# Conditioning projections in rounds of sixteen chunks, four chunks of columns per group of PE columns

## The chip, the cores and the metric

The kernel runs on one core of one Trainium2 chip. Its time is the device time of one launch, in microseconds (us). A core has five engines with queues of their own, which run in order: PE (matmuls; its weight loads are listed as PEld), DVE (vector work), ACT (scalar work), POOL (GpSimd) and SP, which here issues the transfers between main memory (HBM) and the on-chip buffer (SBUF). PE writes into the eight banks of PSUM, and DVE and ACT read results from there. The instructions are ordered on each queue by a scheduler when the program is built, from the order of the code, from priorities (`tc.high_priority`) and from its own simulated times. A tile from a pool with `bufs=n` gets the buffer that was handed out n tiles earlier, and its first writer waits until all readers of that older tile are done.

## What is computed

One inference step of a two-layer decoder for 512 prompt tokens and 8 short sequences of 8 tokens (576 columns in all): a gated delta rule layer (layer A), shared keys and values, and a differential attention layer (layer B). Every norm is shifted and scaled, and every residual gated, by vectors that come from a conditioning input `c`, one row for the prompt and eight for the sequences:

```python
def ada_split(c, w, b, n):
    return jnp.split(c @ w + b, n, axis=-1)

def modulate(x, gain, shift, scale):
    return rms_norm(x, gain) * (1 + scale[:, None, :]) + shift[:, None, :]

shift, scale, gate = ada_split(c, p['ada_w_a'][l], p['ada_b_a'][l], 3)
h = modulate(x, p['norm_a'][l], shift, scale)
```

The three weight matrices have 1024 rows and 3072, 2048 and 3072 columns: 64 chunks of 128 columns. The first 16 (shift and scale of layer A) are needed at once. The change is about the other 48, whose results are first read in the output projection of layer A and later.

## The kernel before

Activations are kept transposed (128 features by 576 columns, eight times). A large projection goes by chunks of 128 output columns (`loadw`, `part`): a raw 512 KB tile `wraw` is loaded, ACT casts it to `whi` (L233), POOL makes the rest `wlo` = `wraw` - `whi` (L234), and PE runs 48 matmuls of 288 columns (L257: for each half of the columns and each of eight row blocks, whi with the high and the low part of the activations, then wlo). There are 105 such chunks in a fixed order of use; `wraw`, `whi` and `wlo` have two buffers each, so the load of a chunk waits for POOL to be done with the chunk before the last.

Layer A (`phase_a`) goes through eight groups of two heads. Strings of letters give the order of the code for a group: `v w z y k q` are projection chunks (v, w, z, y of this group, k and q of the next), `T` and `t` the inverse of a triangular matrix on DVE (`tinv_dve`, L916 and L918 are its inner steps), `P` its completion by small matmuls on PE (`tinv_pe`, L940 to L959, with ACT copies between its stages), `1` and `2` the preparation of the next group (`prep1`: transposes of k and q, L713 to L728, and norms; `prep2`: products of k and q, L757 to L768, from which the next `T` starts), `C` the recurrence over four chunks of the group before, `s r` the eight sequences, `o` its norm and gate, `h` a chunk of the output projection, and `a` one conditioning chunk. `P` takes its PSUM tiles from the pool `pa` (one bank), as the conditioning chunks do; `prep1`, `prep2` and the transposes of v (L788) use the pool `pt` (two banks).

One `a` is `ada_unit`: a 512 KB load into `araw` (L265); eight matmuls (L269), the 32-row conditioning block as weights and 128 columns of the chunk streaming, each on one of the four groups of 32 PE columns, so that the four groups hold four partial sums; an ACT copy out of PSUM (L272); one matmul with a constant of nine columns (L273), which adds up the four partial sums and transposes; a DVE add of the bias (L275) into `mod`.

Of the kernel before, what the change touches and what calls it, by code (L numbers as in the profile page):

```python
# [10 lines left out]
F32 = mybir.dt.float32  # L11
# [4 lines left out]
ALU = mybir.AluOpType  # L16
# [21 lines left out]
VEC = {}  # L38
# [61 lines left out]
    return out  # L100


STEP = 'CvTtwkaaasaazPaqry12o'
STEP0 = 'CTtvaaawazasryakqa12oPa'
STEP7 = 'CTtvswzyaHahhrhhhaahhaaaPoah'
STEP8 = 'CLsaraoaaaaaaaa'


def step_of(i):

    return STEP0 if i == 0 else STEP8 if i == G else STEP7 if i == G - 1 else STEP


CHUNKS = chunk_cols()
WORDER = use_order()
# [91 lines left out]
def scr(K, n):  # L207
    t = K.scr.tile([128, 640], F32, name="scr")
    return t[:, 0:n]
# [48 lines left out]
                               start=(k == 0 and a + b == 0), stop=(k == 7 and a == 1))  # L258


def ada_unit(K, kt, pool, name, raw=None):

    nc = K.nc
    ch = raw or K.araw.tile([128, 8, 128], F32, name="araw")
    nc.sync.dma_start(out=ch[:], in_=K.ada[kt].rearrange("p (k m) -> p k m", m=128))  # L265
    ps = pool.tile([128, 512], F32, name=name)
    for k in range(8):
        j = k % 4
        nc.tensor.matmul(out=ps[32 * j:32 * j + 32, 0:128], lhsT=K.cT[:, k, :], rhs=ch[:, k, :],  # L269
                         start=(k < 4), stop=(k >= 4), tile_position=(0, 32 * j))  # L270
    sb = K.adsb.tile([128, 128], F32, name="adsb")
    nc.scalar.copy(out=sb[:], in_=ps[:, 0:128])  # L272
    nc.tensor.matmul(out=ps[:, 128:137], lhsT=sb[:], rhs=K.asel, start=True, stop=True)  # L273
    v0 = VEC["ada_b"][0] + kt
    nc.vector.tensor_scalar(out=K.mod[:, kt, :], in0=ps[:, 128:137], scalar1=K.vec[:, v0:v0 + 1], scalar2=None,  # L275
                            op0=ALU.add)


def ada_pair(K, k, pool, name, raw):
# [235 lines left out]
def phase_a(K, A, ctx, first):  # L515
    nc = K.nc
    tc = K.tc
    A.rows = ctx.enter_context(tc.tile_pool(name="rows", bufs=1))
    c = load_con(K, A.rows, K.con_in, "mask", "smaskb")
# [10 lines left out]
    def pool(name, bufs):  # L530
        return ctx.enter_context(tc.tile_pool(name=name, bufs=bufs))
# [6 lines left out]
    A.y = pool("y", 1)  # L538
    A.v = pool("v", 1)
    K.araw = pool("araw", 1)  # L540
    K.adsb = pool("adsb", 1)
    A.ln = pool("ln", 1)
    A.gb = pool("gb", 2)
    A.eg = pool("eg", 4)
# [12 lines left out]
    kts = K.kts  # L557

    def ada(raw=None):
        if kts:  # L560
            ada_unit(K, kts.pop(0), K.pa, "pa", raw)
# [7 lines left out]
    ada()  # L569
    ada()  # L570
    prev, cur = None, nxt
    m = 0
    for i in range(G + 1):
        nxt = Group(K, A, i + 1) if i + 1 < G else None
        hot = HP if i == G else 0
        for t in step_of(i):
# [45 lines left out]
            if t == "L":  # L622
                new_h(K)
                out_heads(K, range(8, 14), CUTS)
            if t in "ab":
                ada(A.WFs[0] if t == "b" else None)
        prev, cur = cur, nxt


# [300 lines left out]
def tinv_pe(K, A, ck, WF):  # L930

    nc = K.nc
    XA, XC, WC = A.XA, A.XC, A.WC
    pvz = K.pa.tile([128, 2, 8, 32], F32, name="pa")
    pv, pz = pvz[:, 0], pvz[:, 1]
    V1 = A.ln.tile([128, 8, 32], F32, name="V1", tag="V")
    for s in range(2):
        a, b = 64 * s, 64 * s + 32
        for n in range(8):
            nc.tensor.matmul(out=pv[b:b + 32, n, :], lhsT=ck[a:a + 32, n, b:b + 32], rhs=XC[a:a + 32, n, :],  # L940
                             start=True, stop=True, tile_position=(a, b))
        nc.scalar.activation(out=V1[b:b + 32], in_=pv[b:b + 32], func=AF.Copy, scale=-1.0)
        for n in range(8):
            nc.tensor.matmul(out=pz[a:a + 32, n, :], lhsT=V1[b:b + 32, n, :], rhs=WC[b:b + 32, n, :],
                             start=True, stop=True, tile_position=(b, a))
            if s == 0:
                nc.tensor.matmul(out=pz[b:b + 32, n, :], lhsT=WC[b:b + 32, n, :], rhs=V1[b:b + 32, n, :],
                                 start=True, stop=True, tile_position=(b, b))
        nc.scalar.copy(out=WF[a:a + 32, :, b:b + 32], in_=pz[a:a + 32])
        if s == 0:  # L950
            nc.scalar.copy(out=XA[b:b + 32, :, 0:32], in_=pz[b:b + 32])
    pv2 = K.pa.tile([128, 8, 64], F32, name="pa")
    for n in range(8):
        nc.tensor.matmul(out=pv2[64:128, n, :], lhsT=ck[0:64, n, 64:128], rhs=XA[0:64, n, :],
                         start=True, stop=True, tile_position=(0, 64))
    V2 = A.ln.tile([128, 8, 64], F32, name="V2", tag="V")
    nc.scalar.activation(out=V2[64:128], in_=pv2[64:128], func=AF.Copy, scale=-1.0)
    for n in range(8):
        nc.tensor.matmul(out=pv2[0:64, n, :], lhsT=V2[64:128, n, :], rhs=WF[64:128, n, 64:128],  # L959
                         start=True, stop=True, tile_position=(64, 0))  # L960
# [513 lines left out]
def phase_b(K, ctx, x1, rstd, norm_rest):  # L1474
    nc = K.nc
    tc = K.tc
    P = Ctx()

    def pool(name, bufs):
# [5 lines left out]
    c = load_con(K, one, K.con_in, "amask", "plain")  # L1485
# [11 lines left out]
                            scalar2=None, op0=ALU.mult)  # L1497
# [4 lines left out]
    for t in P.qs + [P.zb]:  # L1502
# [17 lines left out]
                                   op0=ALU.mult, op1=ALU.add)  # L1520
# [15 lines left out]
    for i in (1, 0):  # L1536
# [7 lines left out]
    assert not K.kts  # L1544
    qctx = ExitStack()
    extra_w(K, qctx, "qx", [("b", h * 128) for h in range(2, QH)])
    tiles = []
# [34 lines left out]
    with ExitStack() as pctx:  # L1582
# [10 lines left out]
        n = dict.fromkeys("vzf", 0)  # L1593
# [87 lines left out]
def setup(K, ctx, ins):  # L1681
    nc = K.nc
    tc = K.tc
    K.per = ctx.enter_context(tc.tile_pool(name="per", bufs=1))
    K.wraw = ctx.enter_context(tc.tile_pool(name="wraw", bufs=2))
    K.wq, K.wnext, K.wx = [], 0, {}
    K.g1 = {}
    K.kts = list(range(16, 24)) + list(range(40, 56)) + list(range(24, 40)) + list(range(56, 64))
# [11 lines left out]
    c = load_con(K, K.per, ins["con"], "ident", "asel")  # L1700
# [11 lines left out]
    K.mod = K.per.tile([128, 64, 9], F32, name="mod")  # L1712
    K.wall = ins["wall"]
    K.ada = ins["ada"]
    K.cst_in = ins["cst"]
    K.st_in = ins["st"]
    K.con_in = ins["con"]
# [65 lines left out]
def arrays_of(i):  # L1783
    f = {k: np.asarray(v) for k, v in i.items()}
    xa = np.concatenate([f["x_prompt"].reshape(SEQ, D), f["x_sample"].reshape(NS, D)], 0)
    a = {}
# [6 lines left out]
    a["ada"] = np.ascontiguousarray(ad.reshape(8, 128, 64, 128).transpose(2, 1, 0, 3)).reshape(64, 128, 1024)  # L1793
# [72 lines left out]
```

## Time and profile before

Three runs took 1361.96, 1363.52 and 1375.33 us. The profile is of one further execution.

| what | value |
|---|---|
| median of the runs | 1363.52 us |
| the profiled execution, own time | 1368.16 us |
| its span (first to last instruction) | 1366.4 us |
| mean granted PE clock | 0.953 of full |
| stretch of layer A's groups | about 62 to 760 us |
| conditioning chunks of `ada_unit` in it | 48, from 62 to 676 us |
| `wraw` loads | 105 of 512 KB, median 3.8 us to landing |

A row of instructions gives engine, line, operation, tile written <- tiles read, shape, how many (x), the busy time in us and the mean length of one in ns, then the idle time of the engine just before and what ended it. A row of the timeline gives the start and the length in us. A 32-bit matmul leaves two records (two passes). Matmuls are pipelined, so that two successive starts tell more of what one costs PE than its length.

### The profile page before, as it was taken

What the parts mean: (1) busy time and instruction counts of PE and PEld (TensorE: products, weight loads), DVE (VectorE), ACT (ScalarE), POOL (GpSimd) and SP (SyncE); (2) the same over time, 40 slices, a digit from 0 to 9 for tenths busy, and PEclk for the clock granted to TensorE, in tenths of its full rate; (3) what the DMA queues carried; (4) which work ended last, traced back from release to release, by engine and by line L of the source; (5) the groups of instructions that cost most, each with busy time, mean ns of one, the idle gap of its engine ahead of it and who ended that gap; (6) DMA issues with size and microseconds to landing.
All of it is one profiled execution on the core that took longest, in us unless ns stands there. A gap on an engine that the chain in (4) does not pass through costs nothing.

```text
span 1366.4 us, 31102 instructions
## 1 busy us (share of the span) xinstructions
PE 1256.5 (92%) x11477; PEld 1078.5 (79%) x11477; DVE 961.3 (70%) x2437; ACT 729.1 (53%) x2043; POOL 512.2 (37%) x766
## 2 busy tenths in 40 slices
PE   7989799899899898999889899699999999989988
PEld 4879779688788777978779688599888777767888
DVE  5689986779989788897882668688742466555451
ACT  4566446748576674857643542254444465555440
POOL 4543414224252322424123432945553343423222
PEclk8999889899999999998899899899999999999999
DMA  9353224334334343344444445021777877885333
GB/s 356 134 161 111 83 93 132 112 109 126 134 100 142 118 143 109 116 147 135 125 158 133 149 139 190 31 79 60 263 271 242 260 226 248 284 264 168 114 118 114
DMA packets 79578, 211.63 MB, mean 155 GB/s; under 512 B 13554, under 2 KB 27250, under 8 KB 79426
## 3 DMA queue, kind: packets, MB, share of 16 engines
q1 hardware_dynamic: 79426, 209.64, 47.1%
q8 instruction: 91, 1.49, 0.4%
q14 instruction: 61, 0.50, 0.1%
HBM read 183.76 MB, written 25.84 MB: 153 GB/s over the span
## 4 chain that ended last, share of the span: by engine, by line
PE 53%; DVE 27%; ACT 7%; DMA 5%; issue 5%; POOL 3%; SPq 1%; POOLq 0%; DVEq 0%; ACTq 0%
PE pp L257 26%; DVE y L476 3%; DVE tp L916 3%; PE po L1325 2%; PE pS L1282 2%; DVE XT L918 2%; DMA pg<-ck 2%; PE sc L257 1%; PE pv L1445 1%; PE sc L1405 1%; PE px L1307 1%; PE ps L1023 1%; DMA pg<-cv 1%; PE pa L269 1%; PE pt L757 1%
## 5 line engine op out<-in xcount | busy, mean ns | idle before, releaser
L257 PE MATMUL pp<-hhi,whi 128*128 128x288 f32 x1504 | 460.6, 309 | 29.8 <-ACT hhi L369 12.2
L257 PE MATMUL pp<-hlo,whi 128*128 128x288 f32 x1504 | 456.0, 304 | 2.3 <-DVE hlo L361 1.4
L257 PE MATMUL pp<-hhi,wlo 128*128 128x288 f32 x1504 | 453.5, 302 | 0.3 <-POOL wlo L234 0.3
L234 POOL TENSOR_TENSOR wlo<-wraw,whi 128x1024 fp32r<-128x1024 f32 x105 | 253.4, 2414 | 293.2 <-ACT whi L233 276.5
L257 PEld LDWEIGHTS pp<-hhi,whi 128*128 128x128 f32 x1504 | 285.5, 191 | 48.0 <-ACT hhi L369 12.9
L257 PEld LDWEIGHTS pp<-hlo,whi 128*128 128x128 f32 x1504 | 286.9, 191 | 14.1 <-issue 6.5
L257 PEld LDWEIGHTS pp<-hhi,wlo 128*128 128x128 f32 x1504 | 286.6, 191 | 7.1 <-issue 5.5
L233 ACT CAST whi<-wraw 128x1024 fp32r<-128x1024 f32 x105 | 109.8, 1046 | 104.6 <-PE pp L257 70.2
L476 DVE SCALAR_TENSOR_TENSOR y<-u,vec,y 128x600 f32<-128x600 f32 x96 | 96.4, 1004 | 8.3 <-ACT y L474 7.8
L1051 POOL TENSOR_TENSOR wm<-w,con_mask 96x512 fp32r<-96x512 f32 x32 | 35.4, 1105 | 141.5 <-DVE w L1040 84.5
L916 DVE TENSOR_TENSOR tp<-XT,LA 128x32 f32<-128x32 f32 (+15 forms) x128 | 75.5, 590 | 2.5
L1425 DVE TENSOR_REDUCE mx<-sc 128x1 f32<-128x128 f32 (+3 forms) x64 | 31.4, 491 | 61.1 <-PE sc L1407 61.0
L1252 POOL COPY pg<-ptt 1x1 int32<-1x1 int32 x128 | 27.8, 225 | 104.0 <-PE po L1325 45.4
L918 DVE TENSOR_REDUCE XT<-tp 128x16 f32<-128x32 f32 (+15 forms) x128 | 54.9, 429 | 2.4
L1048 ACT ACTIVATE Ss<-Ss,egl 128x128 f32<-128x128 f32 x128 | 42.2, 395 | 23.7 <-PE ps L1023 23.4
L1325 PE MATMUL po<-pg,pTs 128*8 128x128 f32 x1024 | 42.4, 280 | 4.3 <-DMA pg<-cv 3.8
L1282 PE MATMUL pS<-pg,qs 128*32 128x128 f32 x1024 | 42.5, 278 | 4.2 <-DMA pg<-ck 4.1
L1402 POOL TENSOR_TENSOR qd<-qT,qd 64x128 fp32r<-64x128 f32 x64 | 32.4, 507 | 35.9 <-ACT qd L1401 32.2
L269 PE MATMUL pa<-araw,cT 128*32 128x128 f32 x768 | 35.9, 294 | 8.7 <-DVE mod L275 5.6
L479 ACT ACTIVATE scr<-y 128x600 f32<-128x600 f32 x32 | 22.5, 704 | 36.3 <-DVE y L476 36.0
L1427 ACT ACTIVATE pm<-sc,mx 128x128 f32<-128x128 f32 (+3 forms) x64 | 33.6, 527 | 13.9 <-DVE mx L1425 13.0
L1282 PEld LDWEIGHTS pS<-pg,qs 128*32 128x32 f32 x1024 | 26.8, 109 | 12.8 <-issue 5.1
(455 smaller groups left out, 2772.1 us busy)
## 6 DMA issues: line engine op xcount, KB each, us to landing
wraw<-wall SPq DMA_DIRECT2D x105, 512.0 KB, 3.8
pg<-ck SPq DMA_DIRECT2D x64, 512.0 KB, 5.1
pg<-cv SPq DMA_DIRECT2D x64, 512.0 KB, 4.7
araw<-ada SPq DMA_DIRECT2D x48, 512.0 KB, 3.5
araw<-ada SPq DMA_DIRECT2D x8, 1024.0 KB, 11.9
Ss<-st SPq DMA_DIRECT2D x16, 512.0 KB, 3.7
o_sts<-Ss SPq DMA_DIRECT2D x16, 512.0 KB, 2.9
gb<-gcd SPq DMA_DIRECT2D x16, 288.0 KB, 4.0
```

The costliest lines, as they stand in the source:

```text
L233: nc.scalar.copy(out=hi[:], in_=raw[:])
L234: nc.gpsimd.tensor_sub(out=lo[:], in0=raw[:], in1=hi[:].bitcast(F32))
L257: K.nc.tensor.matmul(out=ps[:, :HT], lhsT=w[a][:, k, :], rhs=h[b][:, k, half * HT:half * HT + HT], start=(k == 0 and a + b == 0), stop=(k ...
L269: nc.tensor.matmul(out=ps[32 * j:32 * j + 32, 0:128], lhsT=K.cT[:, k, :], rhs=ch[:, k, :], start=(k < 4), stop=(k >= 4), tile_position=(0, ...
L476: (nc.gpsimd if j in TAP[K.tapi] else nc.vector).scalar_tensor_tensor(out=y[:, :YW], in0=u[:, j:j + YW], scalar=cw[j], in1=y[:, :YW], op0= ...
L916: nc.vector.tensor_mul(out=tp[:, :, :, :n], in0=XT[:, :, :n].unsqueeze(2).to_broadcast([128, 8, 2, n]), in1=LA[:, i:n, :n].unsqueeze(1).to ...
L918: nc.vector.tensor_reduce(out=XT[:, :, i:n], in_=tp[:, :, :, :n], axis=AX.X, op=ALU.add, negate=True)
L1048: nc.scalar.activation(out=S[:, b, :], in_=S[:, b, :], func=AF.Copy, scale=egl[:, hh, 4 + b:5 + b])
L1051: nc.gpsimd.tensor_mul(out=wm[:], in0=w3[:, a, :].bitcast(F32).unsqueeze(1).to_broadcast([96, 4, 128]), in1=K.smaskb.unsqueeze(2).to_broad ...
L1282: nc.tensor.matmul(out=S[32 * j:32 * j + 32, 128 * pg:128 * pg + 128], lhsT=qs[:, h, :], rhs=kp[:, h, :], start=(hh == 0), stop=(hh == 1), ...
L1325: nc.tensor.matmul(out=po[32 * j:32 * j + 8, hf, :], lhsT=pTs[:, pg, 8 * h:8 * h + 8], rhs=vp[:, h, :], start=False, stop=(pg == NPG - 1 a ...
L1427: nc.scalar.activation(out=p[:, :w], in_=pss[m][:, :w], func=AF.Exp, bias=mx[:, m:m + 1], accum_out=ls[:, qt, m:m + 1])
```

## The change

The 48 chunks go in three rounds of 16. A step (`ada_step`, 24 in all) loads 1 MB: one block of 128 rows of W for the 16 chunks of the round, laid out by the host. It runs four matmuls of 512 columns, one on each group of 32 PE columns, so that each group holds four whole chunks and adds over the eight steps of a round in the one bank of `pa`, which is held through the round. Only the last step of a round copies the bank (ACT, 512 columns, into a tile of the pool `scr`), transposes it in four pieces on PE (L286), and adds the bias on DVE in two pieces. Before, each of the 48 chunks had its own copy, matmul and add.

As `pa` is held, `tinv_pe` takes its two tiles from `pt`. As `araw` is twice as large, `wraw` has one buffer in place of two. Over the eight groups the letter `a` stood 62 times, with two calls ahead of the loop (64 calls, of which the first 48 found work); now it stands 23 times with one call ahead, 24 steps. The other letters keep their order. The 16 first chunks are untouched.

```diff
-STEP = 'CvTtwkaaasaazPaqry12o'
-STEP0 = 'CTtvaaawazasryakqa12oPa'
-STEP7 = 'CTtvswzyaHahhrhhhaahhaaaPoah'
-STEP8 = 'CLsaraoaaaaaaaa'
+STEP = 'CvTtwkasazPaqry12o'
+STEP0 = 'CTtvawazsryakq12oP'
+STEP7 = 'CTtvswzyaHhhrhhhahhPoh'
+STEP8 = 'CLsro'
...
-def ada_unit(K, kt, pool, name, raw=None):
-    ch = raw or K.araw.tile([128, 8, 128], F32, name="araw")
-    nc.sync.dma_start(out=ch[:], in_=K.ada[kt].rearrange("p (k m) -> p k m", m=128))
-    ps = pool.tile([128, 512], F32, name=name)
-    for k in range(8):
-        j = k % 4
-        nc.tensor.matmul(out=ps[32 * j:32 * j + 32, 0:128], lhsT=K.cT[:, k, :], rhs=ch[:, k, :],
-                         start=(k < 4), stop=(k >= 4), tile_position=(0, 32 * j))
-    sb = K.adsb.tile([128, 128], F32, name="adsb")
-    nc.scalar.copy(out=sb[:], in_=ps[:, 0:128])
-    nc.tensor.matmul(out=ps[:, 128:137], lhsT=sb[:], rhs=K.asel, start=True, stop=True)
-    v0 = VEC["ada_b"][0] + kt
-    nc.vector.tensor_scalar(out=K.mod[:, kt, :], in0=ps[:, 128:137], scalar1=K.vec[:, v0:v0 + 1], scalar2=None,
-                            op0=ALU.add)
+def ada_step(K, pool, name):
+    r, k = divmod(K.adn, 8)
+    K.adn += 1
+    ch = K.araw.tile([128, 4, 512], F32, name="araw")
+    nc.sync.dma_start(out=ch[:], in_=K.adb[r, k].rearrange("p (j n) -> p j n", j=4))
+    if k == 0:
+        K.adp = pool.tile([128, 512], F32, name=name)
+    ps = K.adp
+    for j in range(4):
+        nc.tensor.matmul(out=ps[32 * j:32 * j + 32, :], lhsT=K.cT[:, k, :], rhs=ch[:, j, :], start=(k == 0), stop=(k == 7),
+                         tile_position=(0, 32 * j))
+    if k < 7:
+        return
+    sb = scr(K, 512)
+    nc.scalar.copy(out=sb, in_=ps[:])
+    for q in range(4):
+        nc.tensor.transpose(out=ps[:, 128 * q:128 * q + 128], in_=sb[:, 128 * q:128 * q + 128], identity=K.ident)
+    for i in range(2):
+        kt = KTS[ROUND * r + 8 * i]
+        v0 = VEC["ada_b"][0] + kt
+        nc.vector.tensor_add(out=K.mod[:, kt:kt + 8, :].rearrange("p (j q) c -> p j q c", j=2),
+                             in0=fr(ps[:, 64 * i:64 * i + 1], [[32, 2], [128, 4], [1, 9]]),
+                             in1=fr(K.vec[:, v0:v0 + 1], [[4, 2], [1, 4], [0, 9]]))
...
-    pvz = K.pa.tile([128, 2, 8, 32], F32, name="pa")
+    pvz = K.pt.tile([128, 2, 8, 32], F32, name="pt")
...
-    pv2 = K.pa.tile([128, 8, 64], F32, name="pa")
+    pv2 = K.pt.tile([128, 8, 64], F32, name="pt")
...
-    K.wraw = ctx.enter_context(tc.tile_pool(name="wraw", bufs=2))
+    K.wraw = ctx.enter_context(tc.tile_pool(name="wraw", bufs=1))
```

How the change moves instructions is shown at two places. The first is PE around the end of `P` of group 3 and the preparation of group 4 (of groups 0 to 7). Before, the products of `prep2` (L757, tile pt) stand around the last stage of `P` (L959, tile pa), and the transposes of k and q are long past:

```order
L257 MATMUL pp<-hhi,whi 128x288
L257 MATMUL pp<-hlo,whi 128x288
L757 MATMUL pt<-k 128x128
L757 MATMUL pt<-q,k 128x128
L757 MATMUL pt<-k 128x128
L959 MATMUL pa<-WF_131,V_4656 64x64 x8
L757 MATMUL pt<-q,k 128x128
L883 MATMUL ps<-con_ident,osb 128x64
L768 MATMUL pt<-kqs 64x128
L257 MATMUL pp<-hhi,wlo 128x288
```

After, on the same engine, the transposes of k (now L725) stand just ahead of the last stage of `P` (now L971, tile pt):

```order
L260 MATMUL pp<-hhi,whi 128x288
L890 MATMUL ps<-con_ident,ob 128x128 x2
L725 MATMUL pt<-con_ident,k 128x128 x4
L971 MATMUL pt<-WF_131,V_4330 64x64 x8
L890 MATMUL ps<-con_ident,ob 128x128 x2
L260 MATMUL pp<-hlo,whi 128x288
```

Twenty projection matmuls later on PE the transposes of q (L735) and of the sequences' k and q (L740) follow and then `prep2` (L769). The row of a conditioning step (L279, four matmuls) is cut in two here; of the 24 steps, 8 are cut in two parts, 16 stand whole:

```order
L260 MATMUL pp<-hhi,wlo 128x288
L279 MATMUL pa<-araw,cT 32x512 x2
L835 MATMUL pc<-vr,WF_131 128x128 x2
L735 MATMUL pt<-con_ident,q 128x128 x4
L740 MATMUL pt<-con_ident,kqs 128x128
L895 MATMUL ps<-con_ident,osb 128x64
L279 MATMUL pa<-araw,cT 32x512 x2
L843 MATMUL pc<-wv,ckq 128x128 x2
L844 MATMUL pc<-wk,kt 128x256
L1035 MATMUL ps<-Ss,kTm 32x128 x14
L769 MATMUL pt<-k 128x128
```

So `P`, which stood beside the preparation of the next group, now stands ahead of all of it. The second place is SP at the start of the program. Before, the raw tiles of two weight chunks are issued one behind the other:

```order
L283 DMA araw_322<-ada 128x2x1024
L230 DMA wraw<-wall 128x1024 x2
L283 DMA araw_442<-ada 128x2x1024
L283 DMA araw_490<-ada 128x2x1024
L666 DMA cso<-cst 128x4x24 x2
L1017 DMA Ss<-st 128x1024
L283 DMA araw_538<-ada 128x2x1024
L283 DMA araw_586<-ada 128x2x1024
L230 DMA wraw<-wall 128x1024 x2
```

After, one raw tile is issued there, and the second behind all loads of the first sixteen conditioning chunks:

```order
L299 DMA araw_322<-ada 128x2x1024
L233 DMA wraw<-wall 128x1024
L299 DMA araw_442<-ada 128x2x1024
L299 DMA araw_490<-ada 128x2x1024
L678 DMA cso<-cst 128x4x24 x2
L1029 DMA Ss<-st 128x1024
L299 DMA araw_538<-ada 128x2x1024
L299 DMA araw_586<-ada 128x2x1024
L233 DMA wraw<-wall 128x1024
L274 DMA araw<-adb 128x2048
```

The second weight chunk moved from beside the first to behind the last conditioning load.

More of the change, by code (lines that the diff above doesn't have):

```diff
@@ L556, in phase_a, with ada @@
     A.WC = A.ln.tile([128, 8, 32], F32, name="WC")
[L557 to L561, printed above, removed]
+    def ada():
+        ada_step(K, K.pa, "pa")
     nxt = Group(K, A, 0)
@@ L568, in phase_a @@
         nxt.prep2()
-    ada()
     ada()
@@ L624, in phase_a @@
                 out_heads(K, range(8, 14), CUTS)
-            if t in "ab":
-                ada(A.WFs[0] if t == "b" else None)
+            if t == "a":
+                ada()
         prev, cur = cur, nxt
@@ L1543, in phase_b @@
         tabs.append(tab)
-    assert not K.kts
+    assert K.adn == len(KTS) // 2
     qctx = ExitStack()
@@ L1792, in arrays_of @@
     ad = np.concatenate([f["ada_w_a"][0], f["ada_w_kv"], f["ada_w_b"][0]], 1)
-    a["ada"] = np.ascontiguousarray(ad.reshape(8, 128, 64, 128).transpose(2, 1, 0, 3)).reshape(64, 128, 1024)
+    ad = ad.reshape(8, 128, 64, 128)
+    a["ada"] = np.ascontiguousarray(ad[:, :, :16].transpose(2, 1, 0, 3)).reshape(16, 128, 1024)
+    a["adb"] = np.ascontiguousarray(ad[:, :, KTS].reshape(8, 128, 3, 16, 128).transpose(2, 0, 1, 3, 4)).reshape(3, 8, 128, 2048)
     W = {"a": f["w_in_a"][0], "oa": f["w_out_a"][0], "kv": f["w_kv"], "b": f["w_in_b"][0], "ob": f["w_out_b"][0]}
```

6 lines of the change are left out of this document (4 added, 2 removed).

## The prediction

> **What bounds the kernel now.** I read the page's engine table and chain first, then windows, then groups by line, then the timeline of PE and DVE where the edits stand. Engine, busy time, share and instructions; then the shares of the chain of work that ended last:
>
> ```profile
> PE 1256.5 (92%) x11477; PEld 1078.5 (79%) x11477; DVE 961.3 (70%) x2437; ACT 729.1 (53%) x2043; POOL 512.2 (37%) x766
> PE 53%; DVE 27%; ACT 7%; DMA 5%; issue 5%; POOL 3%; SPq 1%; POOLq 0%; DVEq 0%; ACTq 0%
> ```
>
> PE is busy for 92%, yet only 53% of the chain is PE's and 27% is DVE's: a microsecond taken from PE does not arrive whole. By stretch (its length; busy PE, PEld, DVE, ACT, POOL; granted clock; DMA share; GB/s), first all groups of layer A, then its beginning, then one group:
>
> ```profile
> 62.00:760.00 698.00, 640.99 (x5720) 560.06 (x5718) 574.46 (x1449) 429.95 (x1298) 234.63 (x275) 0.95 0.39 124
> 62.00:180.00 118.00, 102.10 (x889) 91.36 (x888) 109.08 (x243) 69.65 (x193) 47.76 (x57) 0.91 0.36 112
> 343.00:421.00 78.00, 73.22 (x710) 65.13 (x712) 69.33 (x180) 54.92 (x170) 27.21 (x35) 0.98 0.41 131
> ```
>
> The first 118 us are led by DVE (109 of 118), later groups by PE (73 of 78) with DVE close behind (69). PE stands idle for 698 - 641 = 57 us in the stage. The conditioning chunks hold these groups there (busy, mean ns, then idle time ahead and what ended it):
>
> ```profile
> L269 PE MATMUL pa<-araw,cT 128*32 128x128 f32 x768 | 35.9, 294 | 8.7 <-DVE mod L275 5.6 <-DMA araw<-ada 3.1
> L273 PE MATMUL pa<-con_ident,adsb 128*128 128x9 f32 x96 | 15.5, 234 | 1.1 <-ACT adsb L272 1.0
> L275 DVE TENSOR_SCALAR mod<-pa,vec 128x9 f32<-128x9 f32 x48 | 10.5, 218 | 4.8 <-PE pa L273 4.7
> ```
>
> **PE work removed.** Pipelined matmuls are priced by how far they push the next start. One chunk's eight matmuls, and then its summing matmul, between projection matmuls:
>
> ```profile
> 61.92 0.29 PE L257 MATMUL pp<-hlo,whi 128*128 128x288 f32 x1
> 62.14 0.64 PE L269 MATMUL pa<-araw,cT 128*32 128x128 f32 x16
> 62.71 0.40 PE L257 MATMUL pp<-hhi,wlo 128*128 128x288 f32 x1
> ...
> 66.39 0.30 PE L257 MATMUL pp<-hhi,wlo 128*128 128x288 f32 x1
> 66.53 0.30 PE L257 MATMUL pp<-hhi,whi 128*128 128x288 f32 x1
> 66.66 0.28 PE L273 MATMUL pa<-con_ident,adsb 128*128 128x9 f32 x2
> 66.80 0.38 PE L257 MATMUL pp<-hlo,whi 128*128 128x288 f32 x1
> 67.02 0.29 PE L257 MATMUL pp<-hhi,wlo 128*128 128x288 f32 x1
> ```
>
> The usual pitch is 66.53 - 66.39 = 0.14. The chunk costs 62.71 - 61.92 - 0.13 = 0.66. From 66.53 to 67.02 are 0.49 with two pitches of 0.13 in them, so L273 costs 0.23. 48 x 0.89 = 42.7 us go.
>
> **PE work added.** The nearest rows to a step of four by 512 columns are the sixteen first chunks (256 columns wide), whose row also shows the same work packed four wide; the others are a chunk that PE's order cuts in two, and four transposes of 128 columns:
>
> ```profile
> 44.51 1.93 PE L287 MATMUL pt<-araw,cT 128*32 128x256 f32 x32
> ...
> 357.08 0.62 PE L269 MATMUL pa<-araw,cT 128*32 128x128 f32 x10
> 358.05 0.42 PE L269 MATMUL pa<-araw,cT 128*32 128x128 f32 x6
> 374.64 0.66 PE L723 MATMUL pt<-con_ident,q 128*128 128x128 f32 x4
> ```
>
> 32 records are two such chunks of eight matmuls in two passes: 0.97 us for 8 x 256 columns, as many as 4 x 512. With the 0.1 that a switch cost above (0.66 against the record's 0.64, and a longer first pass behind it) a step takes 1.07, and 24 take 25.7. The low end is 24 x 0.90 = 21.6, if longer streams hide the weights better; the high end is 24 x 1.93 = 46, if two of the four passes do not overlap; 0.97 is nearest, being of the same columns on the same four groups.
>
> By the order of after, 8 of the 24 steps are cut in two pairs with other matmuls between. The chunk cut above took 0.62 + 0.42 = 1.04 against 0.64 whole, as groups overlap only where they stand together. A cut step then keeps its two pairs busy for a whole stream each: + 0.97, times 8 = 7.8 (from 0, if the neighbours fill in, to 8). Twelve transposes at 0.66 / 4 to 0.27: 2.0 to 3.2, taken 2.6. Added: 25.7 + 7.8 + 2.6 = 36.1; PE saves 6.6.
>
> A rule bears on the step. The Trainium skill, "TensorE: Matmul & The Clock Gate", Part 3 on packing small matmuls, gives 2.38 for three column tiles of 32 by 512, 79% of the ideal 3. By it a step would take 0.97 / 0.79 = 1.23, an estimate, and the sum would rise by 24 x 0.26 = 6. No run here shows four groups at 512 columns; the 128-wide and 256-wide rows agree on almost full overlap (0.64 for 128 x 8, 1.93 for 256 x 16), so I keep 0.97.
>
> **Idle time and other engines.** The waits at L269 of 5.6 (for L275 to leave the one bank) and 3.1 (for `araw`, one buffer) and of 1.1 at L273 are per chunk; three rounds in place of 48 leave few of the first. The loads of 1 MB have a row from the start of the program (median time to landing last):
>
> ```profile
> araw<-ada SPq DMA_DIRECT2D x8, 1024.0 KB, 11.9
> ```
>
> 24 steps in a stage of 698 us stand 29 us apart, so 11.9 is hidden there, as long as two steps stand no closer than that; where the order puts them closer, PE waits for the rest, up to 11 us once a group. I take 6 of 9.8 as saved; 0 is possible, if PE then waits for DVE or for such a load, and 9.8 at most. DVE loses 10.5 for six longer adds (at the 0.22 of L275 to about 0.5: 1.3 to 3), ACT 48 small copies for three. So PE and its waits lose 12.6. What arrives at the end: in the first stretch, where DVE leads, little; some 40 of the 48 chunks stand in groups led by PE, where DVE is 4 us of 78 behind. I take 8; from 0 to 12.6.
>
> **`P` on `pt`, and the preparation behind it.** T is the DVE inverse of group 3 (its first and last inner steps, and the first of group 4); then `P` and the preparation of group 4, in time:
>
> ```profile
> 342.88 0.18 DVE L916 TENSOR_TENSOR tp<-XT,LA 128x32 f32<-128x32 f32 x1
> 369.72 0.68 DVE L916 TENSOR_TENSOR tp<-XT,LA 128x512 f32<-128x512 f32 x1
> 379.00 0.39 PE L273 MATMUL pa<-con_ident,adsb 128*128 128x9 f32 x2
> 383.42 0.69 PE L940 MATMUL pa<-XC,ckq 32*32 32x32 f32 x16
> 395.20 0.27 PE L728 MATMUL pt<-con_ident,kqs 128*128 128x128 f32 x1
> 408.62 1.14 PE L959 MATMUL pa<-WF,V 64*64 64x64 f32 x16
> 410.22 1.66 DVE L761 SCALAR_TENSOR_TENSOR ckq<-pt,sj,gb 128x256 f32<-128x256 f32 x4 [1.93 <-PE pt L757]
> 421.30 0.18 DVE L916 TENSOR_TENSOR tp<-XT,LA 128x32 f32<-128x32 f32 x1
> ```
>
> The loop from T to T is 421.30 - 342.88 = 78.4 us. Before, `P` starts 13.0 us after T's last products (370.4 to 383.4), behind a conditioning chunk in `pa` until 379.4, and runs beside the transposes of k and q, which use `pt`. After, `pa` no longer stops it, but in the order of after the transposes of k stand just ahead of `P`'s last stage, and q's and `prep2` behind it. `P` lasts 383.4 to 409.8 = 26.4; from the last transpose to the end of the products of `prep2` go 411.9 - 395.2 = 16.7; in sequence 43. Between T's end and the next T lie 50.9. So it just fits if `P` starts within 8 us of T's end, and if it starts at 13 the next T is late by 5 to 6 us a group: at most + 36 over six groups. If `P` starts 8 to 13 us earlier and `prep2` follows sooner, up to 13 are gained in all, since PE and DVE, at 73 and 69 of 78, leave no more. I take + 0.7 a group, + 4: nearer to zero than the middle of -13 to +36, since the products of `prep2` moved forward with `P`. The queue behind `P`'s first matmul on PE holds projections and the recurrence of the group before; they wait as before.
>
> **One `wraw` buffer.** A load may start only once POOL is done with the chunk before. The load's row (median landing last), then POOL and ACT at the end of the program, at its start, and at the first and last of ten casts in the output projection of layer A:
>
> ```profile
> wraw<-wall SPq DMA_DIRECT2D x105, 512.0 KB, 3.8
> ...
> 1322.52 2.41 POOL L234 TENSOR_TENSOR wlo<-wraw,whi 128x1024 fp32r<-128x1024 f32 x1 [15.49 <-ACT whi L233]
> ...
> 1324.55 1.05 ACT L233 CAST whi<-wraw 128x1024 fp32r<-128x1024 f32 x1 [2.11 <-PE pp L257]
> 1337.39 1.05 ACT L233 CAST whi<-wraw 128x1024 fp32r<-128x1024 f32 x1 [5.31 <-PE pp L257]
> 1350.11 1.05 ACT L233 CAST whi<-wraw 128x1024 fp32r<-128x1024 f32 x1 [5.31 <-PE pp L257]
> ...
> 26.85 1.04 ACT L233 CAST whi<-wraw 128x1024 fp32r<-128x1024 f32 x1
> 26.09 2.38 POOL L234 TENSOR_TENSOR wlo<-wraw,whi 128x1024 fp32r<-128x1024 f32 x1 [0.21 <-ACT whi L233]
> ...
> 774.24 1.04 ACT L233 CAST whi<-wraw 128x1024 fp32r<-128x1024 f32 x1 [1.93 <-PE ps L1042]
> 826.18 1.05 ACT L233 CAST whi<-wraw 128x1024 fp32r<-128x1024 f32 x1 [3.29 <-DMA wraw<-wall]
> ```
>
> The loop becomes 3.8 + 1.05 + 2.39 = 7.24 us a chunk. In the tail PE takes (1350.11 - 1337.39) / 2 = 6.36. There the cast of 1324.55 could come at 1322.52 + 2.41 + 3.8 = 1328.7, 4.2 late; four more chunks lose 0.88 each; a cast stands 6.36 ahead of its use and needs 3.44 with POOL, so 2.9 are slack: 4.2 + 3.5 - 2.9 = + 4.8, taken 4.5 (0 to 7.7). At the start the second cast moves from 26.85 to 26.09 + 2.38 + 3.8 = 32.3: 5.4 late, taken + 2, as DVE leads there (0 to 5.4). In the output projection ten casts come every (826.18 - 774.24) / 9 = 5.77: at worst 9 x 1.47 = + 13; other matmuls stand between, taken + 1. In the groups 48 projection chunks stand in 698 us, 14.5 apart on the mean against 7.24: + 1. On SP's queue a load that waits for POOL holds those behind it, the 1 MB loads among them, for up to 3.44 us (ACT and POOL of one chunk); the 29 us between steps cover that. Sum + 8.5 (0 to 27).
>
> **Sum.** The profiled execution took 1368.2 against a median of 1363.5; the terms are differences, set on the median: 1363.5 - 8 + 4 + 8.5 = 1368; I say 1367.
>
> **Rivals.** First, faster: all 12.6 arrive, and `P` freed from `pa` starts early, and gains its whole 13: 1363.5 - 12.6 - 13 + 8.5 = 1346. For it speaks that L273 of a chunk stands in `P`'s way; against it that DVE hardly gets faster. It decides if `P` starts within 6 us of T's end. Second, slower, by the place of `P` alone: the preparation behind it lengthens the T loop by 5 for five groups: 1363.5 + 25 = 1389. For it speaks the order; it decides once `P` and preparation exceed 50.9. Third, slower by the single landing buffer pacing every dense stretch: 1363.5 - 8 + 24 = 1380, decided where 7.24 exceeds the pitch of the chunks. The Trainium skill, "Trainium Kernel Development and Optimization", Best Practices, asks to double-buffer so that transfers overlap with compute; it speaks for this one, and the trace shows its loop only as a sum of rows. Fourth, no saving, as DVE carries the chain: 1363.5 + 8.5 = 1372.
>
> **Chances.** Forecast 0.35, first rival 0.18, second 0.20, third 0.14, fourth 0.13. The range leaves out the lower half of the first and the upper half of the second: 1347 to 1390. A measurement here tells about 1% from no change, 13.6 us: below 1349.9 lies most of the first case, 0.18; above 1377.1 the second, the third and a little of the forecast, 0.34; between, 0.48.
>
> **What would show it.** Step right: L279 with 24 x about 1 us; wrong: 1.5 or more. `P`: its first small matmul less than 9 us behind T's last products, and T to T at 78 or 79; wrong: 83 or more. `wraw`: casts in the tail 7.2 apart and waiting for the DMA. Saving: the groups end 5 to 10 us before 760. The forecast is wrong if that end moves by more than 15 either way, or if the stretch behind it (output projection, layer B and tail, where only the buffer of `wraw` differs) grows by more than 10.

## The result and the profile after

The changed kernel took 1414.74 us (median of 4 runs, 1413.35 to 1415.74) against 1368.20 us (1361.96 to 1375.33) for the kernel before on the same chip: a ratio of 1.0353 with a 95% interval of 1.0318 to 1.0389. It is slower by 3.5% of 1368, about 48 us (46.5 between the medians), and 25 above the upper end of the range. Its profiled execution has a span of 1413.0 us.

The engine table, the chain of waits and its costliest lines, from the page of the kernel after (in this file L260 is the projection matmul, L236 ACT's cast, L237 POOL's subtraction):

```profile
PE 1268.4 (90%) x10817; PEld 1062.1 (75%) x10817; DVE 948.0 (67%) x2395; ACT 723.0 (51%) x1998; POOL 510.9 (36%) x766
...
PE 43%; DVE 21%; DMA 12%; ACT 7%; POOL 6%; issue 4%; SPq 0%; POOLq 0%; ACTq 0%; DVEq 0%
PE pp L260 21%; DMA wraw<-wall 6%; POOL wlo L237 3%; DVE y L492 3%; ACT whi L236 2%; PE pS L1294 2%; DMA pg<-cv 2%; DMA pg<-ck 2%; PE po L1337 2%; PE ps L1035 2%; DVE tp L928 1%; PE sc L260 1%; DVE gb L713 1%; PE sc L1417 1%; PE pv L1457 1%
```

No engine works more than before, apart from 12 us on PE, and those are no added work: the matmuls of the projection chunks in tile pp, the same 4512, take 1383.6 us in sum against 1370.1, at a mean granted clock of 0.943 against 0.953. PE's share of the chain falls from 53 to 43%, DMA's rises from 5 to 12 and POOL's from 3 to 6. Three of the lines, the load of `wraw`, ACT's cast and POOL's subtraction, are the loop through the single landing buffer: together 11%. One group of instructions tells it best, ACT's casts, with the idle time ahead of them (before, then after):

```profile
L233 ACT CAST whi<-wraw 128x1024 fp32r<-128x1024 f32 x105 | 109.8, 1046 | 104.6 <-PE pp L257 70.2 <-issue 14.8 <-DMA wraw<-wall 10.5
```

```profile
L236 ACT CAST whi<-wraw 128x1024 fp32r<-128x1024 f32 x105 | 109.9, 1047 | 163.4 <-DMA wraw<-wall 105.8 <-PE pp L260 50.9 <-issue 4.9
```

The waits for the load rise from 10.5 to 105.8 us. The second loss is in layer A's groups. The same rows as in the prediction, of T of group 3, `P`, and the preparation of group 4, after:

```profile
341.30 3.33 DVE L928 TENSOR_TENSOR tp<-XT,LA 128x32 f32<-128x32 f32 x1
371.65 1.84 DVE L928 TENSOR_TENSOR tp<-XT,LA 128x512 f32<-128x512 f32 x1
380.83 0.69 PE L952 MATMUL pt<-XC,ckq 32*32 32x32 f32 x16
404.33 0.60 PE L725 MATMUL pt<-con_ident,k 128*128 128x128 f32 x4
404.86 1.14 PE L971 MATMUL pt<-WF,V 64*64 64x64 f32 x16
410.90 0.27 PE L740 MATMUL pt<-con_ident,kqs 128*128 128x128 f32 x1
418.34 3.22 DVE L773 SCALAR_TENSOR_TENSOR ckq<-pt,sj,gb 128x256 f32<-128x256 f32 x8
433.01 0.18 DVE L928 TENSOR_TENSOR tp<-XT,LA 128x32 f32<-128x32 f32 x1
```

`P` starts 7.3 us behind T's end (before: 13.0), but the transposes of k wait until its last stage, and the products of the preparation end at 421.6, 15.6 us behind `P`; before, both ended within 2.1 us. From T to the next T are 91.7 us, 13 more than before in this group.

Where the time is lost can be read from when ACT casts a given weight chunk, since the 105 chunks have the same order in both. The table is from the timelines of ACT; its middle columns are two of the experiments below, in each of which one part of the change is made alone:

| chunk, and what it belongs to | before | `P` on `pt` alone | one `wraw` alone | after |
|---|---|---|---|---|
| 57, end of layer A's groups | 737.4 | +15.1 | +0.8 | +24.6 |
| 69, end of the output projection | 826.2 | +13.3 | +18.7 | +46.1 |
| 73, layer B | 899.1 | +14.2 | +10.3 | +38.6 |
| 97, ahead of the tail | 1281.5 | +11.2 | +6.9 | +30.6 |
| 105, the last | 1350.1 | +11.1 | +25.2 | +49.7 |

These are single profiled executions, and that of before lies some 3 us above the median of its runs, those of the two parts alone some 2 below theirs, so that the columns understate each loss a little. Both shifts that the prediction named as signs of an error are there: the end of the groups is 24.6 us later, where 15 were the limit, and the stretch behind it 25 us longer, where 10 were.

### The profile page after: what moved, and what is told of

Read it like the earlier page. It is cut to its first block, busy times and chain, and to the rows that moved or that the text cites. A ratio compares the mean times of both kernels' runs of the same rounds, so it can differ in the third digit from the quotient of the medians.

```text
span 1413.0 us, 29592 instructions
## 1 busy us (share of the span) xinstructions
PE 1268.4 (90%) x10817; PEld 1062.1 (75%) x10817; DVE 948.0 (67%) x2395; ACT 723.0 (51%) x1998; POOL 510.9 (36%) x766
## 4 chain that ended last, share of the span: by engine, by line
PE 43%; DVE 21%; DMA 12%; ACT 7%; POOL 6%; issue 4%; SPq 0%; POOLq 0%; ACTq 0%; DVEq 0%
PE pp L260 21%; DMA wraw<-wall 6%; POOL wlo L237 3%; DVE y L492 3%; ACT whi L236 2%; PE pS L1294 2%; DMA pg<-cv 2%; DMA pg<-ck 2%; PE po L1337 2%; PE ps L1035 2%; DVE tp L928 1%; PE sc L260 1%; DVE gb L713 1%; PE sc L1417 1%; PE pv L1457 1%
## 5 line engine op out<-in xcount | busy, mean ns | idle before, releaser
L260 PE MATMUL pp<-hhi,whi 128*128 128x288 f32 x1504 | 466.1, 312 | 40.7 <-ACT hhi L385 12.8
L260 PE MATMUL pp<-hlo,whi 128*128 128x288 f32 x1504 | 460.3, 307 | 4.7 <-DVE hlo L1098 2.5
L260 PE MATMUL pp<-hhi,wlo 128*128 128x288 f32 x1504 | 457.2, 305 | 4.7 <-POOL wlo L237 4.6
L237 POOL TENSOR_TENSOR wlo<-wraw,whi 128x1024 fp32r<-128x1024 f32 x105 | 255.3, 2431 | 376.9 <-ACT whi L236 355.4
L260 PEld LDWEIGHTS pp<-hhi,whi 128*128 128x128 f32 x1504 | 289.4, 193 | 69.3 <-ACT hhi L385 14.2
L260 PEld LDWEIGHTS pp<-hhi,wlo 128*128 128x128 f32 x1504 | 289.6, 193 | 18.6 <-issue 8.0
L260 PEld LDWEIGHTS pp<-hlo,whi 128*128 128x128 f32 x1504 | 290.4, 193 | 17.1 <-issue 6.4
L236 ACT CAST whi<-wraw 128x1024 fp32r<-128x1024 f32 x105 | 109.9, 1047 | 163.4 <-DMA wraw<-wall 105.8
L1035 PE MATMUL ps<-Ss,kTm 128*32 128x128 f32 x512 | 39.8, 295 | 0.6 <-DVE Ss L1067 0.6
L1294 PEld LDWEIGHTS pS<-pg,qs 128*32 128x32 f32 x1024 | 25.7, 109 | 15.4 <-issue 7.8
```

Source lines behind the costliest of these rows:

```text
L236: nc.scalar.copy(out=hi[:], in_=raw[:])
L237: nc.gpsimd.tensor_sub(out=lo[:], in0=raw[:], in1=hi[:].bitcast(F32))
L260: K.nc.tensor.matmul(out=ps[:, :HT], lhsT=w[a][:, k, :], rhs=h[b][:, k, half * HT:half * HT + HT], start=(k == 0 and a + b == 0), stop=(k ...
L1035: nc.tensor.matmul(out=pa[p:p + 32, 0, :], lhsT=A.kTm[:, i, a, b4, :], rhs=S[:, 4 * a + b4, :], start=(b4 == 0), stop=(b4 == 3), tile_posi ...
L1294: nc.tensor.matmul(out=S[32 * j:32 * j + 32, 128 * pg:128 * pg + 128], lhsT=qs[:, h, :], rhs=kp[:, h, :], start=(hh == 0), stop=(hh == 1), ...
```

## The experiments

Each edit is scheduled anew, so that instructions move in places that the edit doesn't name: the rest of a group can shift by some 10 us (with one `wraw` alone, T of group 2 starts at 259.3 us against 268.7 before). The edits are shown shortened. Ratios are to the kernel before on the same chip, with 95% intervals.

**One landing buffer alone.** In the kernel before:

```diff
-    K.wraw = ctx.enter_context(tc.tile_pool(name="wraw", bufs=2))
+    K.wraw = ctx.enter_context(tc.tile_pool(name="wraw", bufs=1))
```

> The kernel before with one buffer of wraw in place of two, nothing else. Theory W (the single landing buffer makes nearly all of the loss): +35 to +55 us on the kernel before, that is a ratio of 1.026 to 1.040, and the chain of waits shows DMA wraw, ACT whi and POOL wlo. Rival P (P on the shared pool and the preparation behind it make layer A's share of 25 us): only the part behind layer A, +15 to +25, ratio 1.011 to 1.018. Rival S (the steps themselves cost more than the chunks): under +15.

Measured 1392.86 us, 1.0227 [1.0180, 1.0273]: some 31 us, between what theory W and rival P asked for. So the buffer makes a large part of the loss, not all. ACT's casts in the output projection of layer A, the kernel before and then this one:

```profile
774.24 1.04 ACT L233 CAST whi<-wraw 128x1024 fp32r<-128x1024 f32 x1 [1.93 <-PE ps L1042]
775.52 1.04 ACT L233 CAST whi<-wraw 128x1024 fp32r<-128x1024 f32 x1
782.25 1.04 ACT L233 CAST whi<-wraw 128x1024 fp32r<-128x1024 f32 x1 [1.67 <-DMA wraw<-wall]
790.07 1.04 ACT L233 CAST whi<-wraw 128x1024 fp32r<-128x1024 f32 x1
792.36 1.04 ACT L233 CAST whi<-wraw 128x1024 fp32r<-128x1024 f32 x1
...
817.65 1.05 ACT L233 CAST whi<-wraw 128x1024 fp32r<-128x1024 f32 x1 [1.71 <-PE pt L257]
821.49 1.05 ACT L233 CAST whi<-wraw 128x1024 fp32r<-128x1024 f32 x1 [2.33 <-DMA wraw<-wall]
826.18 1.05 ACT L233 CAST whi<-wraw 128x1024 fp32r<-128x1024 f32 x1 [3.29 <-DMA wraw<-wall]
```

```profile
799.23 1.04 ACT L233 CAST whi<-wraw 128x1024 fp32r<-128x1024 f32 x1 [3.21 <-DMA wraw<-wall]
806.29 1.05 ACT L233 CAST whi<-wraw 128x1024 fp32r<-128x1024 f32 x1 [5.67 <-DMA wraw<-wall]
813.40 1.05 ACT L233 CAST whi<-wraw 128x1024 fp32r<-128x1024 f32 x1 [0.97 <-DMA wraw<-wall]
820.60 1.05 ACT L233 CAST whi<-wraw 128x1024 fp32r<-128x1024 f32 x1 [4.05 <-DMA wraw<-wall]
```

With two buffers the casts come in pairs, 1.3 to 4 us apart, with longer pauses; with one they keep step at 7.1 us, each waiting for its load. The mean of the first (5.77) hides that the second buffer was a store, filled in the pauses.

**`P` on `pt` alone.** In the kernel before:

```diff
-    pvz = K.pa.tile([128, 2, 8, 32], F32, name="pa")
+    pvz = K.pt.tile([128, 2, 8, 32], F32, name="pt")
...
-    pv2 = K.pa.tile([128, 8, 64], F32, name="pa")
+    pv2 = K.pt.tile([128, 8, 64], F32, name="pt")
```

> The kernel before with the two tiles of tinv_pe from pt in place of pa, nothing else. Theory W: no change, ratio 0.995 to 1.005. Rival P: +15 to +30 us, ratio 1.011 to 1.022, with T to T longer than 78 us in the groups of layer A.

Measured 1381.28 us, 1.0135 [1.0093, 1.0176]: rival P's price, about 18 us. The two alone sum to 31 + 18 = 49 us; the whole change costs 48. From T of group 1 to T of group 7 there are six periods; the first inner steps of both, before, in this kernel, and after:

```profile
170.94 0.18 DVE L916 TENSOR_TENSOR tp<-XT,LA 128x32 f32<-128x32 f32 x1
...
664.58 3.17 DVE L916 TENSOR_TENSOR tp<-XT,LA 128x32 f32<-128x32 f32 x1
```

```profile
167.85 0.74 DVE L916 TENSOR_TENSOR tp<-XT,LA 128x32 f32<-128x32 f32 x1
...
685.96 0.18 DVE L916 TENSOR_TENSOR tp<-XT,LA 128x32 f32<-128x32 f32 x1
```

```profile
165.62 0.36 DVE L928 TENSOR_TENSOR tp<-XT,LA 128x32 f32<-128x32 f32 x1
...
691.59 2.11 DVE L928 TENSOR_TENSOR tp<-XT,LA 128x32 f32<-128x32 f32 x1
```

The mean period is 82.3 us before, 86.4 with `P` on `pt` and 87.7 after; with one `wraw` alone it is 81.9. What `pt` does to the order is seen in group 3: before, the first transposes of k for group 4 ran at 352 us, 31 us ahead of `P`; in this kernel they wait until `P`'s last stage, and the products of the preparation follow (first line before, then this kernel):

```profile
352.48 1.09 PE L713 MATMUL pt<-con_ident,k 128*128 128x128 f32 x4
```

```profile
385.89 0.60 PE L713 MATMUL pt<-con_ident,k 128*128 128x128 f32 x4
386.42 1.14 PE L959 MATMUL pt<-WF,V 64*64 64x64 f32 x16
407.41 3.22 DVE L761 SCALAR_TENSOR_TENSOR ckq<-pt,sj,gb 128x256 f32<-128x256 f32 x8
```

The products end 23.1 us behind `P` (387.6 to 410.6). In groups 1 to 6 they end 16 to 24 us behind `P`, before between 6 ahead and 8 behind. From T's end to their end a group takes 49.0 us in the mean against 46.6 before, 15 us over six groups. T itself is longer by 9 us in sum, in group 5 alone by 14 (39.4 against 25.0); why stays open.

**Two landing buffers in the kernel after.** To make room, a step's 1 MB goes in two loads into a tile of half the size:

```diff
+    for e in range(2):
+        ch = K.araw.tile([128, 4, 256], F32, name="araw")
+        nc.sync.dma_start(out=ch[:], in_=K.adb[r, k, :, 1024 * e:1024 * e + 1024].rearrange("p (j n) -> p j n", j=4))
+        for j in range(4):
+            nc.tensor.matmul(out=ps[32 * j:32 * j + 32, 256 * e:256 * e + 256], lhsT=K.cT[:, k, :], rhs=ch[:, j, :], ...)
...
-    K.wraw = ctx.enter_context(tc.tile_pool(name="wraw", bufs=1))
+    K.wraw = ctx.enter_context(tc.tile_pool(name="wraw", bufs=2))
```

> The kernel after with two buffers of wraw; to make room, a step's 1 MB goes as two loads of 512 KB into a tile of half the size, and as two times four matmuls of 256 columns on the same four groups. Theory W: back to the kernel before or a little under it, ratio 0.99 to 1.005. Rival P: layer A still 25 us late, ratio 1.015 to 1.022. Rival S: ratio over 1.022.

Measured 1384.58 us, 1.0141 [1.0097, 1.0185]. The same half steps with the single buffer are the control:

> The same half steps with the single buffer of wraw: tells whether the half steps alone change anything. All theories: within 10 us of the kernel after, ratio 1.028 to 1.043 on the kernel before; a ratio far below it would mean that the 1 MB loads were part of the loss.

Measured 1419.81 us, 1.0405 [1.0358, 1.0452]. The half steps cost at most a little (1.0405 against 1.0353, intervals overlapping), and the second buffer alone gives back 35 us. The row of casts shows it: the wait for the load is 7.4 us.

```profile
L236 ACT CAST whi<-wraw 128x1024 fp32r<-128x1024 f32 x105 | 109.7, 1046 | 124.4 <-PE pp L260 71.0 <-issue 35.5 <-DMA wraw<-wall 7.4
```

What is left, 1.4%, is as much as `P` on `pt` costs alone (1.0135), with the steps in this kernel: theory W's claim to the whole falls.

**The preparation ahead of `P`, both on `pt`.** In the kernel with `P` on `pt`:

```diff
-STEP = 'CvTtwkaaasaazPaqry12o'
+STEP = 'CvTtwkaaasaazaq12Pryo'
```

> The kernel before with P's two tiles from pt, as in the run that took 1.0135, and the letters q, 1 and 2 (the next group's q chunk and preparation) ahead of P in the code. Theory O (the loss of P on pt is the order: in a shared pool the preparation gets its buffers in the order of the code, so that it stands behind P): k's transposes stand early in T again, T to T falls from 86 to about 82 and the ratio to 0.99 to 1.006. Rival B (the loss is the two buffers themselves: P's tiles hold them while ACT copies, whoever comes first): 1.010 to 1.020.

Measured 1430.55 us, 1.0470 [1.0396, 1.0545]: worse than either foresaw. T of group 4 ends, the preparation of group 5 goes through, and `P` of group 4 starts only behind it (last inner step of T, last products of the preparation, first matmuls of `P`):

```profile
463.29 0.68 DVE L916 TENSOR_TENSOR tp<-XT,LA 128x512 f32<-128x512 f32 x1
523.70 1.26 DVE L761 SCALAR_TENSOR_TENSOR ckq<-pt,sj,gb 128x256 f32<-128x256 f32 x3
...
525.10 1.03 PE L940 MATMUL pt<-XC,ckq 32*32 32x32 f32 x16 [1.01 <-DVE mod L275]
```

`P` now comes 61 us behind T (464.0 to 525.1). So the order alone is not what is wrong: two stretches of work that share a pool of two buffers take their buffers in the order of the code, and the second waits for the first, whichever it is. On separate banks, as before, they ran beside each other. In groups 1 to 6 the wait is 49 to 69 us.

**Weight chunks in halves.** In the kernel after, each chunk is loaded, cast and split in two halves of 256 KB through two landing buffers of half the size:

```diff
+    for e in range(2):
+        s = slice(4 * e, 4 * e + 4)
+        raw = K.wraw.tile([128, 4, 128], F32, name="wraw")
+        nc.sync.dma_start(out=raw[:], in_=K.wall[ci][:, 512 * e:512 * e + 512].rearrange("p (k m) -> p k m", m=128))
+        nc.scalar.copy(out=hi[:, s, :], in_=raw[:])
+        nc.gpsimd.tensor_sub(out=lo[:, s, :], in0=raw[:], in1=hi[:, s, :].bitcast(F32))
```

> The kernel after with each weight chunk loaded, cast and split in two halves of 256 KB, with two landing buffers of half the size, so that the memory stays that of one buffer. Theory W (the loop of load, ACT and POOL through one buffer costs some 30 us): the halves overlap and most of it comes back, ratio 1.010 to 1.020 on the kernel before; casts in the tail 6.4 us apart again. Rival F (what counts is the second buffer's full chunk of lookahead, or the smaller pieces cost ACT and POOL as much): ratio over 1.027.

Measured 1383.07 us, 1.0112 [1.0038, 1.0186]: 33 of 48 us come back in the same memory. With the preparation ahead of `P` as well:

> The kernel after with the half landing buffers and with q, 1 and 2 ahead of P: undoes both losses and keeps the steps. If theories W and O hold and their effects add: ratio 0.985 to 1.005, which shows what the steps themselves are worth. Rivals B and F together: over 1.02.

Measured 1424.23 us, 1.0420 [1.0347, 1.0492]: the same harm as in the other kernel with that order.

**No conditioning chunks at all.** In the kernel before, the list of the 48 chunks is left empty, so that this kernel leaves out part of the result.

> The kernel before without the 48 conditioning chunks (their loads, matmuls, copies and adds are left out; the vectors are set to zero). Tells what their PE time is worth at the end, an upper bound for any saving. Theory D (DVE and the loop of T, P and preparation carry the groups): at most 15 us faster, ratio 0.989 to 1.0. Rival E (PE carries them): 40 to 55 us faster, ratio 0.960 to 0.971.

Measured 1349.76 us, 0.9872 [0.9804, 0.9941]: a little more than theory D allowed (0.989) and far from rival E. All of their work, on PE put at 42.7 us with 9.8 us of waits, is worth 17 us (8 to 27) at the end. That contains what `P` gains from a free `pa`: it starts 5 to 11 us behind T's end in groups 1 to 6, before 5 to 35. The groups in that kernel (columns as in the prediction):

```profile
62.00:700.00 638.00, 566.39 (x4579) 501.27 (x4578) 549.46 (x1368) 404.76 (x1208) 220.16 (x268) 0.92 0.28 90
```

PE is busy for 566 of 638 us and DVE for 549, so that neither fills the groups; with so little won by 42.7 us less on PE, this fits theory D's loop of T, `P` and preparation, which no run takes away. The granted clock of these runs was 0.937 to 0.943, that of the kernel before beside them 0.941 to 0.959, so that part of the gain may have gone there.

**Rounds between one `P` and the next.** So that `P` can have `pa` again, a round's eight steps are written behind `P` of groups 1, 3 and 5 and ahead of the following `P`; the weights go in halves:

```diff
-STEP = 'CvTtwkasazPaqry12o'
+STEP = 'CvTtwkszPaqary1a2ao', 'CvaTtwakasazPqry12o'
```

> The kernel after with the half landing buffers of the weights, with P's tiles back on pa, and with each round of eight steps written between one P and the next (four steps behind P of groups 1, 3 and 5, four ahead of P of groups 2, 4 and 6), so that pa is free at every P. The theory that the loss was P against the preparation in pt plus the single landing buffer, and that the steps themselves cost no more than the chunks: ratio 0.985 to 1.004; T to T back at 82 us or less. Rival (eight steps so close together wait for their loads, or P waits for the end of a round): 1.005 to 1.02.

Measured 1381.70 us, 1.0143 [1.0096, 1.0190]: the rival's number, with 82.8 us from T to T in the mean. The same with two whole landing buffers and half steps:

> The same places of P and the rounds, with two whole landing buffers for the weights and half steps (two loads of 512 KB, 256 columns). Same theory: 0.985 to 1.006, and beside the run before it tells whether halves of the weights or halves of the steps cost less. Rival as before: 1.005 to 1.02.

Measured 1437.98 us, 1.0546 [1.0507, 1.0586], far above both ranges. Its conditioning matmuls, with the idle time ahead of them:

```profile
L280 PE MATMUL pa<-araw,cT 128*32 128x256 f32 x384 | 42.2, 516 | 52.6 <-DMA araw<-adb 52.5
```

Sixteen loads close together through one small buffer hold PE for 52.5 us, and with the round `pa`, so that `P` of group 4 starts 38 us behind T's end (463.3 to 501.8). And with the single landing buffer and whole steps:

> The kernel after with only P and the rounds moved in the same way: the single landing buffer of the weights stays. If the two losses add, the loss of P's place (16 us) goes and that of the landing buffer (30 us) stays: ratio 1.015 to 1.026. If the place of P was only a part that hid behind the landing buffer: over 1.03.

Measured 1402.83 us, 1.0268 [1.0218, 1.0318]: against 1.0353 some 12 us come back, less than the 18 of `P` alone; in group 4, where `P` stands behind a round, it starts 19 us behind T's end (431.7 to 451.1), which may be the rest. This lies just above the range for two losses that add, and below that of the rival (1.03).

**Whole landing buffers behind layer A.** The rounds between one `P` and the next, with halves only in layer A's groups:

```diff
+            K.wraw, K.wn = actx.enter_context(tc.tile_pool(name="wraw", bufs=2)), 4
...
+            K.wraw, K.wn = bctx.enter_context(tc.tile_pool(name="wraw", bufs=2)), 8
```

> The kernel of the rounds between P's (1.0143) with the half landing buffers only while layer A's groups run, and two whole ones from the output projection of layer A on. If the half chunks are what still costs there (its groups end 19 us ahead of the kernel before, its end is 11 late): ratio 0.993 to 1.007. Rival (an earlier end of the groups is lost in what follows, whatever the buffers): 1.010 to 1.018.

Measured 1378.41 us, 1.0115 [1.0068, 1.0162]: no different from 1.0143, in the rival's range. And halves in the kernel before, with nothing else:

> The kernel before with its weight chunks in two halves of 256 KB through two landing buffers of half the size, nothing else. If the half chunks cost what the run of the rounds between P's shows behind layer A: ratio 1.005 to 1.013. Rival (halves with two buffers hide the load as whole ones do): 0.997 to 1.004.

Measured 1381.72 us, 1.0128 [1.0084, 1.0173]: halves do cost, some 17 us, at the top of the first case's range. Their price in ACT and POOL is in their rows in the kernel after with halves:

```profile
L238 ACT CAST whi<-wraw 128x512 fp32r<-128x512 f32 x210 | 122.6, 618 | 156.7 <-PE pp L262 79.1 <-DMA wraw<-wall 62.8 <-issue 4.5
...
L239 POOL TENSOR_TENSOR wlo<-wraw,whi 128x512 fp32r<-128x512 f32 x210 | 279.8, 1347 | 351.7 <-ACT whi L238 330.5 <-PE pp L262 10.9 <-PE ps L897 5.0
```

Halves take 26 us more of POOL than whole chunks (279.8 against 253.4) and ACT still waits 62.8 us for loads. None of the versions that compute the whole result beats the kernel before.

## Why the prediction was wrong, point by point

**The steps on PE: right.** A whole step between projection matmuls, after:

```profile
459.13 0.29 PE L260 MATMUL pp<-hhi,wlo 128*128 128x288 f32 x1
459.34 1.06 PE L279 MATMUL pa<-araw,cT 128*32 128x512 f32 x8
460.34 0.40 PE L260 MATMUL pp<-hhi,whi 128*128 128x288 f32 x1
```

It pushes the next start by 460.34 - 459.13 - 0.13 = 1.08 us; the forecast was 1.07. Eight of the 24 were cut in two, as the order said, and each part of these takes 1.04 to 1.06, so that the row's 35.0 us are 1.46 a step; with 2.5 for the transposes that makes 37.5 against the 36.1 of the forecast. The rule of the Trainium skill, "TensorE: Matmul & The Clock Gate", Part 3, would have given 1.23, an estimate; four column groups at 512 columns overlap more fully here. Nor were the 1 MB loads a cost: they landed in 4.9 us, and PE waited 0.8 us for them:

```profile
L279 PE MATMUL pa<-araw,cT 128*32 128x512 f32 x192 | 35.0, 629 | 2.4 <-ACT u L474 1.5 <-DMA araw<-adb 0.8
...
araw<-adb SPq DMA_DIRECT2D x24, 1024.0 KB, 4.9
```

**What arrives of the saving: sized too high.** Of 12.6 us on PE I let 8 arrive. All 48 chunks together are worth 17 of 52 us, a third; at that rate, an estimate, 4 arrive, and the measured sum of the other two terms leaves 49 - 48 = 1, with intervals of some 5 us on each.

**`P` on `pt`: the term of the sum was mis-sized.** + 4 was taken, + 18 measured (13 to 24), inside the -13 to +36 that went with it. The step that failed is the choice, "nearer to zero than the middle of -13 to +36, since the products of `prep2` moved forward with `P`": they moved, but behind `P`. The arithmetic of that paragraph (43 in sequence, 50.9 to hold them) already said that the loop just fits at best, and it was made on one group whose period (78.4) is shorter than the mean of six (82.3). The second rival's mechanism was the true one: 4.1 us a group in the mean with `P` on `pt` alone (86.4 - 82.3), 5.4 after (87.7 - 82.3). Of the six times 4.1 some 15 us are left at chunk 57. My test for `P`, that it starts less than 9 us behind T, came true (7.3) and said nothing, as the preparation behind it is what the next T waits for; the other half of the test, T to T at 78 or 79, failed (91.7 in this group).

**One `wraw`: the term was mis-sized.** + 8.5 was taken, + 31 measured (25 to 37), at or beyond the upper bound of 27. The loop of 7.24 us was right: the last casts of the tail stand 7.3 to 7.5 us apart, each waiting for its load (after):

```profile
1392.37 1.05 ACT L236 CAST whi<-wraw 128x1024 fp32r<-128x1024 f32 x1 [6.32 <-DMA wraw<-wall]
1399.84 1.05 ACT L236 CAST whi<-wraw 128x1024 fp32r<-128x1024 f32 x1 [6.42 <-DMA wraw<-wall]
```

What failed is setting that loop against the mean pitch of the chunks. In the output projection, "other matmuls stand between, taken + 1", the buffer's loss is 18 us at chunk 69 (some 8 of them given back by chunk 73), because the chunks are wanted in pairs; and between chunks 97 and 105, where I took 4.5 for the tail, another 18 are lost, because before, the first chunks of the tail (99 to 101) had landed 12 to 17 us ahead of their casts, and one buffer cannot run ahead so far (alone, 7.4, 4.3 and 0.1 us). The 3 us put for the start and the groups are 0.8 at chunk 57. The Trainium skill, "Trainium Kernel Development and Optimization", Best Practices, asks to double-buffer so that transfers overlap with compute. The runs agree, with 31 us for this buffer.

**Rivals as alternatives.** The second and third rival were given as cases of which one holds, each with its own time. They are at different places and, within the noise, add: 1368 + 18 + 31 = 1417, against 1415 measured. With the prices that I gave them, both at once would have been 1363.5 - 8 + 25 + 24 = 1404.5; the range ended at 1390.

**What stays open.** At chunk 57 the kernel after is 24.6 us late, where the two parts alone give 15.9; whether the steps, the single buffer among them or the new schedule make the other 9 wasn't separated, and the profile of before, above its median, accounts for some 3 of it and the profiles of the two parts, below theirs, for some 4. And in the kernels with the rounds between one `P` and the next, the last `P` ends some 20 us ahead of the kernel before (710.9 and 708.5 against 730.2), but they are 15.4 and 13 us behind it by chunk 57. Whole buffers behind layer A change that little; where the lead goes was not found.

The halves do not add up either. The kernel after with halves has `P` on `pt` (18 us alone) and the halves (17 us alone), and costs 15 in all (1.0112); with `P` back on `pa` it is no faster (1.0143).

The granted clock was not held fixed. In the runs of the kernel before on record, 37 with the profiled one, the time falls from 1379.43 us at 0.941 to 1354.30 at 0.961, by a straight line through all of them 9.3 us per hundredth. The four runs of the kernel after had 0.935 to 0.943, so that some 12 of its 48 us, an estimate by that line, go with a lower clock, and parts of the losses of the two edits alone do as well (0.939 to 0.947 with one `wraw`, 0.943 to 0.952 with `P` on `pt`). Whether the lower clock follows from PE's longer waits or is a loss of its own was not separated; it does not account for ACT's waits for the load or for the steps in the table. The kernel with whole buffers behind layer A ran at 0.933 to 0.943, which by the same line goes with some 12 of the 16 us that it loses.

## What to carry to other kernels

A buffer's worth is not read from the mean pitch of what goes through it: look at the bursts, and at how early its loads landed. Before work is moved into a shared pool, list what else takes buffers there and ask which chains will now exclude one another in the order of the code; a busy share near 90% on one engine does not mean that its work is what bounds the stage, and a run without the work shows at once what a saving can bring. Two losses at different places can both come: here those of the shared pool and of the single buffer added up, and were not to be weighed against each other as alternatives; that of the halves did not add, so that each sum needs its own run.

## What the runs showed of the hardware

Half a chunk takes more than half the time: ACT's cast took 0.618 us for 512 columns (the kernel after with halves) against 1.046 for 1024 (the kernel before), POOL's subtraction 1.347 against 2.414. A load of 1 MB landed in 4.9 us beside layer A's work and in 11.9 among the loads at the start of the program.
